# Three blocks on one core: modulation chunks redistributed around three passages from a norm to its transposes

## The chip, the cores and the metric

The kernel runs on one core of one Trainium2 chip. The metric is device time in microseconds (us) of one execution. Before the change it is 1364.03 us, the median of three runs (1363.72 to 1364.52).

## The reference

The input `x` is 256 tokens by 1024 columns, all in float32. A first block updates it by a mixer, a cross attention to 256 memory tokens and a SwiGLU feed-forward layer, each behind an RMS norm. A second block then runs twice, with its own weights for each of its two layers `l`: a mixer of four parts, and a mixture of 32 experts in groups. Cut to the part that matters here:

```python
mod = silu(c) @ w_ada[l] + b_ada[l]          # 1024 -> 6 x 1024
sh1, sc1, g1, sh2, sc2, g2 = split(mod, 6)
h = rms(x) * norm_mix_g[l] * (1 + sc1) + sh1
x = x + g1 * token_mixer(h, ...)
h = rms(x) * norm_ffn_g[l] * (1 + sc2) + sh2
x = x + g2 * hierarchical_moe(h, ...)
```

The modulation `mod` depends on `c` alone, not on `x`. So its product with `w_ada` (two layers of 1024 by 6144) can be computed at any time before its use.

## The kernel before, in words

**Stages.** In the order of the program: mixer 1, memory attention (`mem_attn`), feed-forward (`ffn`), then for l = 0 and l = 1 the mixer (`mixer2`) and the experts (`moe`), and a last norm. At the start of each stage a norm (`normed`, lines 355 to 364) turns `x` into scaled rows `xn`, half on DVE (line 363) and half on ACT (line 364). `to_T` (line 378) transposes them on TensorE in 16 pieces of 128x128, and ACT and DVE evacuate the pieces into `hT`, each as a high and a low part (lines 383 and 384 in `ffn`, lines 389 to 394 in the mixers). The passage from a norm to these transposes happens three times with work of the modulation nearby: n3 in `ffn`, and n4 in each of the two mixers.

**Products.** A float32 product is made of three matmuls of rounded parts (`mm3`, lines 277 to 279: high by high, high by low, low by high; called a triple below). The weights are split into the two parts on ACT (line 239, `whi`) and DVE (line 241, `wlo`). A product of 128 output rows over the 1024 rows of `hT` takes eight triples.

**Chunks.** `ada` (line 1032) computes the modulation as a generator: for each layer three groups `g`, and for each group eight chunks of `w_ada`, 128x2048 or 1 MB each, 48 in all. A chunk is a load on SP's queue (line 1053) and four matmuls (line 1055). When a group's eight are done, ACT copies its row (line 1060), TensorE makes four transposes (line 1067) and for g > 0 sixteen small matmuls (line 1078), and DVE adds biases (lines 1063, 1069 and 1081). This is called the mod row's work. `fill(n)` lets the generator go n steps at the place in the program where it is called, and `need(l, g)` runs it until a group is there. The table `FILL` (line 124) says how many steps are made where: 10 in `mem_attn` and one more behind it, 10 in `ffn` ahead of `to_T`, 12 in the first mixer ahead of `to_T`, none there in the second, and 7 and 8 within the main loops of the two mixers.

**Loads.** Loads of weights are issued by SP in the order of its queue, each into one of the 8 KB places (per partition) that `wtile` hands out in rotation. A load waits on SP until its place is free, and everything behind it on SP waits with it. In `moe` the places make a ring of slots of three (gate, up and down weights of an expert). `moe` ends with a branch (line 1864) to code for overflowing experts (`overflow`, line 1892 its loop), which has memory of its own.

**Order.** Each engine works its instructions in program order. The framework's scheduler may place a call's instructions ahead of those of an earlier call that wait for data; what results is seen in the order below.

Of the kernel before, what the change touches and what calls it, by code (L numbers as in the profile page):

```python
# [15 lines left out]
P = 128  # L16
S = 256
D = 1024
KT = 8
# [101 lines left out]

FILL = {"mem": 1, "ffn": 10, "mix0": 12, "mix": (7, 8)}

ORDER = (2, 0, 3, 1)

# [11 lines left out]
class Net:  # L139
# [280 lines left out]
    def build(self):  # L420
        ctx, tc, nc = self.ctx, self.tc, self.nc
        pool = lambda n, b, **k: ctx.enter_context(tc.tile_pool(name=n, bufs=b, **k))
        self.cst = pool("cst", 1)
        self.places = []
        self.ring, self.rest = [], []
        self.wctx = ctx.enter_context(ExitStack())
        self.kept = [self.more_places(self.wctx, "wst", 3), self.more_places(self.wctx, "wstb", 2)]
        self.per = pool("per", 1)
        self.junk = pool("junk", 1)
        self.psum = pool("psum", 8, space=bass.MemoryType.PSUM)  # L430
        x = self.per.tile([P, 2, D], F32, name="x")
        xs = self.A["x"][0].rearrange("(t p) d -> p t d", p=P)
        nc.sync.dma_start(x[:, 0], xs[:, 0])
        nc.scalar.dma_start(x[:, 1], xs[:, 1])
        self.x = x
        for tt in range(2):
            for h in range(2):
                self.x_done(tt, h)
        self.mhalf = self.cst.tile([P, 8], F32, name="mhalf")
        nc.gpsimd.memset(self.mhalf, -0.5)  # L440
        con = self.cst.tile([P, NCON1], F32, name="con")
        nc.scalar.dma_start(con, self.A["consts"][:, :NCON1])
        par = self.cst.tile([P, NPAR], F32, name="par")
        nc.scalar.dma_start(par, self.A["params"])
        self.C = {k: con[:, o:o + w] for k, (o, w) in CCOLS.items() if o < NCON1}
        self.V = {k: par[:, o:o + w] for k, (o, w) in PCOLS.items()}
        self.ident = self.C["ident"]
        o = CCOLS["upto"][0]
        self.upto_ones = con[:, o:o + 256]
        self.filler, self.ready = self.ada(), -1  # L450
        self.block1()
        if self.stop == "b1":
            return
        self.block2()
# [485 lines left out]
    def ffn(self):  # L940
        tc, nc, V, A = self.tc, self.nc, self.V, self.A
        v, act, te = nc.vector, nc.scalar, nc.tensor
        c, (self.whl, pf) = self.scope(("whl2", 4), ("pf", 1))
        with c:
            xn = self.normed(pf, "n3")
            self.fill(FILL["ffn"])
            hT = self.hpair(pf)
            win, wout = A["w_ffn_in"][0], A["w_ffn_out"][0]
            NJ = 11
            chunks = []  # L950
            for j in range(NJ + 1):
                if j < NJ:
                    chunks += [(win[:, j * 256:(j + 1) * 256], KT, 256, "n"),
                               (win[:, 2816 + j * 256:2816 + (j + 1) * 256], KT, 256, "n")]
                if j:
                    chunks += [(wout[(j - 1) * 256:j * 256, :], 2, D, "k")]
            hs = self.halves(chunks)
            self.to_T(xn, V["g_ffn_pre"], out=hT)
            ob = self.ob = [[self.bank("ob") for _ in range(2)] for _ in range(2)]

            def down(j, hid):
                for k in range(2):
                    W = next(hs)
                    for tt in range(2):
                        for half in range(2):
                            self.mm3(ob[tt][half], hid[:, k, tt * P:(tt + 1) * P], W[:, 0, half * 512:half * 512 + 512],
                                     j == 0 and k == 0, j == NJ - 1 and k == 1)

            pend = None
            for j in range(NJ + 1):  # L970
                if j < NJ:
                    bks = []
                    for _ in range(2):
                        bk = self.bank()
                        for f in range(2):
                            self.feat(bk[:, f * S:(f + 1) * S], next(hs), 0, P, hT)
                        bks.append(bk)
                if pend:
                    down(*pend)
                    pend = None  # L980
                if j < NJ:
                    bg, bu = bks
                    th = pf.tile([P, 512], F32, name="th", bufs=2)
                    act.activation(th, bg, AF.Tanh, scale=0.5)
                    v.scalar_tensor_tensor(th, th, 1.0, bg, op0=OP.add, op1=OP.mult)
                    v.scalar_tensor_tensor(th, th, 0.5, bu, op0=OP.mult, op1=OP.mult)
                    hid = Split(pf.tile([P, 2, S], F32R, name="hidh", bufs=2), pf.tile([P, 2, S], F32R, name="hidl", bufs=2))
                    t = th.rearrange("p (f t) -> p f t", f=2)
                    act.activation(hid.hi, t, AF.Copy)
                    v.tensor_tensor(hid.lo, t, hid.hi, op=OP.subtract)  # L990
                    pend = (j, hid)
            ss = self.sum_sq(pf, "o3")
            for h in range(2):
                ss.add(h, slice(h * 512, h * 512 + 512), [ob[0][h], ob[1][h]])
            self.post(pf, ss, "g_ffn_post")
        self.dump("x3", self.x)
# [35 lines left out]
    def ada(self):  # L1032
# [3 lines left out]
        nc = self.nc  # L1036
# [5 lines left out]
        for l in range(2):  # L1042
# [6 lines left out]
            for g in range(3):  # L1049
                bk = self.bank("ada")  # L1050
                for k in range(KT):
                    w = self.wtile()
                    nc.sync.dma_start(w, self.A["w_ada_2"][l][k * P:(k + 1) * P, g * 2048:(g + 1) * 2048])
                    for q in range(4):
                        te.matmul(bk[q * 32:(q + 1) * 32, :], cact[:, k:k + 1].to_broadcast([P, 32]),  # L1055
                                  w[:, q * 512:(q + 1) * 512], start=k == 0, stop=k == KT - 1)
                    if k < KT - 1:
                        yield
                row = self.per.tile([P, 512], F32, name="modrow")
                act.activation(row, bk, AF.Copy)  # L1060
                if g:
                    sl = slice(0, 64) if g == 1 else slice(64, 128)
                    v.tensor_tensor(grow[sl], grow[sl], bk[sl], op=OP.add)
                yield
                bk = self.bank()
                for c in range(4):
                    nc.tensor.transpose(bk[:, c * P:(c + 1) * P], row[:, c * P:(c + 1) * P], self.ident)
                cols = lambda t, o: t[:, o + g * 16:o + (g + 1) * 16].rearrange("p (q c) -> p c q", q=4)
                v.tensor_tensor(cols(self.mod[l], 0), bk.rearrange("p (c q r) -> p c q r", c=4, q=4)[:, :, :, 0],
                                cols(self.V["b_ada_2"], l * 48), op=OP.add)  # L1070
                if g:

                    bk = self.bank()
                    twin = row.rearrange("p (i k) -> p k i", k=8)
                    for k in range(8):
                        for h in range(2):
                            q = (2, 0)[g - 1] + h
                            te.matmul(bk[h * 64:h * 64 + 64, k:k + 1], twin[:, k], self.ident[:, q * 32:q * 32 + 1],
                                      start=True, stop=True)
                    o = (16, 40)[g - 1]  # L1080
                    v.tensor_tensor(self.mod[l][:, o:o + 8], bk[:, :8],
                                    self.V["b_ada_2"][:, l * 48 + o:l * 48 + o + 8], op=OP.add)
                self.ready = 3 * l + g

    def need(self, l, g):

# [15 lines left out]
    def mixer2(self, l):  # L1102
        tc, nc, V, C = self.tc, self.nc, self.V, self.C
# [4 lines left out]
        with c:  # L1108
# [8 lines left out]
            with tc.tile_pool(name="pxn2", bufs=1, reuse_waits="tile") as pxn:  # L1117
                xn = self.normed(pxn, "n4")
                with self.behind(2):
                    nc.gpsimd.dma_start(wdt, A["w_dt"][l])  # L1120
                    nc.gpsimd.dma_start(con2, self.A["consts"][:, NCON1:])
                    nc.gpsimd.dma_start(self.wr, A["w_router"][l])
                self.fill(FILL["mix0"] if l == 0 else 0)
                self.need(l, 0)
                self.retire(lambda p: p in self.kept)
                mod = self.mod[l]
# [5 lines left out]
                hs = self.halves([(win[:, c0:c0 + 256], KT, 256, "k" if c0 in (1800, 2824) else "n") for c0 in cols]  # L1132
                                 + [(wo[i], 2, D, "k" if n < 3 else "n") for n, i in enumerate(ORDER)])
                self.to_T(xn, ga, b=mod[:, 0:8], out=hT)
                self.free = 3
            self.top.close()

# [522 lines left out]
    def moe(self, l):  # L1660
# [209 lines left out]
        if l == 0:  # L1870
# [3 lines left out]
            a, b = self.places[4:], self.places[1:4]  # L1874
            self.places = (b + a if low else a + b) + self.places[:1]
            self.top = ExitStack()
        self.dump("x5_%d" % l, x)

    def overflow(self, l, pm, xn, ga, bb, comb, rank, sel):
# [84 lines left out]
```

## Time and profile before

| | |
|---|---|
| time, median of 3 runs | 1364.03 us (1363.72 to 1364.52) |
| the profiled execution's own time | 1362.82 us |
| its span, first to last instruction | 1360.9 us |
| mean granted TensorE clock | 0.957 of full |
| busy: TensorE / DVE / ACT / POOL | 92% / 52% / 41% / 6% |
| DMA moved | 375.93 MB, mean 276 GB/s |

The span leaves out what lies around the first and last instruction, here 1.9 us. A busy TensorE may run at its full clock or at half of it; the granted clock tells which. In the rows below a time is in us from the span's start, the brackets give the idle time of the engine ahead of a row and what ended it, and a count such as x40 counts the passes of the hardware, two for each float32 matmul.

### The profile page before, as it was taken

The numbers are of one execution on the slowest core, as the hardware profiler recorded it, in microseconds if no ns is written. First come the engines' busy times: TensorE is split into PE (matmuls) and PEld (weight loads), VectorE is DVE, ScalarE is ACT, GpSimd is POOL, SyncE is SP. The second block draws the span as 40 slices with busy tenths as digits, with TensorE's granted clock in tenths as the row PEclk, the third lists the DMA queues.
The fourth block names the chain that finished last, engine by engine and source line by source line (L and its number), as shares of the span: only waits on it lengthen the run. The fifth ranks groups of instructions, "written<-read, shape, count | busy, mean of one in ns | idle before, by whom it ended". The sixth has DMA issues, their size and how long they took to land. (4 is left out here: it accounts for less than half of the span.)

```text
span 1360.9 us, 26539 instructions
## 1 busy us (share of the span) xinstructions
PE 1246.7 (92%) x11058; PEld 999.5 (73%) x11058; DVE 702.4 (52%) x1414; ACT 552.3 (41%) x1022; POOL 76.8 (6%) x91
## 2 busy tenths in 40 slices
PE   6999999999999999999989977788999989978886
PEld 6988899866999995788876645465888877645553
DVE  5797756545555554686563322225685553332324
ACT  5578546544444443445532211114345532211212
POOL 2000000000000001122100000001122100000000
PEclk9998999999999998999989999888999989998988
DMA  9553448769955555864368999999563476999994
GB/s 313 166 180 96 167 159 275 303 269 379 365 201 188 186 186 180 296 228 152 142 278 364 418 418 419 418 420 336 175 229 139 171 279 281 418 418 418 418 418 181
DMA packets 131946, 375.93 MB, mean 276 GB/s; under 512 B 7056, under 2 KB 90128, under 8 KB 100848
## 3 DMA queue, kind: packets, MB, share of 16 engines
q1 hardware_dynamic: 130080, 367.84, 71.8%
q0 software_dynamic: 1312, 5.21, 1.0%
q8 instruction: 90, 1.47, 0.4%
q10 hardware_dynamic: 432, 1.14, 0.2%
q14 instruction: 32, 0.26, 0.1%
HBM read 373.12 MB, written 1.05 MB: 275 GB/s over the span
## 5 line engine op out<-in xcount | busy, mean ns | idle before, releaser
L241 DVE TENSOR_TENSOR wlo<-w,whi 128x1024 fp32r<-128x1024 f32 x214 | 263.0, 1231 | 190.0 <-ACT whi L239 189.7
L239 ACT ACTIVATE whi<-w 128x1024 fp32r<-128x1024 f32 x214 | 225.7, 1057 | 269.4 <-PE bk L278 181.2
L277 PE MATMUL bk<-hTh,whi 128*128 128x256 f32 (+1 forms) x1128 | 321.8, 287 | 2.7 <-ACT whi L239 2.5
L278 PE MATMUL bk<-hTl,whi 128*128 128x256 f32 (+1 forms) x1128 | 317.2, 282 | 0.9 <-DVE hTl L384 0.7
L279 PE MATMUL bk<-hTh,wlo 128*128 128x256 f32 (+1 forms) x1128 | 316.3, 281 | 0.3 <-DVE wlo L241 0.2
L277 PEld LDWEIGHTS bk<-hTh,whi 128*128 128x128 f32 (+1 forms) x1128 | 211.5, 188 | 21.4 <-issue 4.1
L1631 PE MATMUL bk<-w,XT 128*32 128x256 f32 (+1 forms) x2816 | 178.1, 410 | 44.9 <-DMA w<-in_w_up 41.0
L278 PEld LDWEIGHTS bk<-hTl,whi 128*128 128x128 f32 (+1 forms) x1128 | 210.9, 187 | 3.4 <-DVE hTl L384 1.2
L279 PEld LDWEIGHTS bk<-hTh,wlo 128*128 128x128 f32 (+1 forms) x1128 | 210.8, 187 | 2.0 <-DVE kk L1421 0.8
L1631 PEld LDWEIGHTS bk<-w,XT 128*32 128x32 f32 x2816 | 100.2, 118 | 121.6 <-issue 72.6
L1760 PE MATMUL bk<-Sg,xn 128*128 128x128 f32 x704 | 90.1, 285 | 4.3 <-DVE Sg L1740 4.3
L1760 PEld LDWEIGHTS bk<-Sg,xn 128*128 128x128 f32 x704 | 87.6, 201 | 6.8 <-issue 5.3
L1815 PE MATMUL bk<-w,hd 128*32 x704 | 79.8, 593 | 9.1 <-DMA w<-in_w_down 5.4
L1803 ACT ACTIVATE hd<-bk 128x256 f32<-128x256 f32 x22 | 8.4, 384 | 192.3 <-PE bk L1801 192.3
L1766 DVE TENSOR_SCALAR XT<-bk,gp,modcol 128x128 f32<-128x128 f32 x88 | 36.1, 410 | 87.3 <-PE bk L1760 79.0
L1822 ACT ACTIVATE oh<-od 128x512 fp32r<-128x512 f32 x44 | 27.7, 629 | 88.0 <-DVE od L1821 88.0
L1815 PEld LDWEIGHTS bk<-w,hd 128*32 128x32 f32 x704 | 23.4, 110 | 53.2 <-issue 49.6
L1793 DVE SCALAR_TENSOR_TENSOR mth<-mth,cslot,bk 128x256 f32<-128x256 f32 x22 | 10.6, 481 | 90.6 <-PE bk L1631 90.6
L1764 ACT ACTIVATE XT<-bk,modcol,gp 128x128 f32<-128x128 f32 x88 | 40.1, 456 | 37.0 <-DVE XT L1766 37.0
L1055 PE MATMUL ada<-w,cact 128*32 128x512 f32 x384 | 52.4, 654 | 1.0 <-DMA w<-in_w_ada 1.0
L1821 DVE TENSOR_TENSOR od<-bk,gb 128x512 f32<-128x512 f32 x44 | 30.2, 687 | 36.0 <-PE bk L1815 36.0
L1823 DVE TENSOR_TENSOR ol<-od,oh 128x512 fp32r<-128x512 f32 x44 | 30.4, 691 | 31.6 <-ACT oh L1822 31.5
(511 smaller groups left out, 1938.1 us busy)
## 6 DMA issues: line engine op xcount, KB each, us to landing
w<-in_w_gate SPq DMA_DIRECT2D x64, 1024.0 KB, 19.9
w<-in_w_up SPq DMA_DIRECT2D x64, 1024.0 KB, 19.9
w<-in_w_down SPq DMA_DIRECT2D x64, 1024.0 KB, 19.9
w<-in_w_in SPq DMA_DIRECT2D x48, 1024.0 KB, 6.6
w<-in_w_ada SPq DMA_DIRECT2D x48, 1024.0 KB, 5.0
w<-in_w_ffn_in SPq DMA_DIRECT2D x22, 1024.0 KB, 11.5
w<-in_w_out SPq DMA_DIRECT2D x12, 1024.0 KB, 5.3
w<-in_w_ffn_out SPq DMA_DIRECT2D x11, 1024.0 KB, 6.8
```

Source lines behind the costliest of these rows:

```text
L239: self.nc.scalar.activation(W.hi, v, AF.Copy)
L241: self.nc.vector.tensor_tensor(W.lo, v, W.hi, op=OP.subtract)
L277: mm(out, l.hi, r.hi, start=start, stop=False)
L278: mm(out, l.hi, r.lo, start=False, stop=False)
L279: mm(out, l.lo, r.hi, start=False, stop=stop)
L1055: te.matmul(bk[q * 32:(q + 1) * 32, :], cact[:, k:k + 1].to_broadcast([P, 32]), w[:, q * 512:(q + 1) * 512], start=k == 0, stop=k == KT - 1)
L1631: self.nc.tensor.matmul(out[ps, :S], XT[:, k, ps], w[i][:, k * S:(k + 1) * S], start=k == 0, stop=k == KT - 1)
L1760: te.matmul(o, xn[:, tt, d], Sg[:, tt], start=tt == 0, stop=tt == 1)
L1764: act.activation(XT[:, d], o, AF.Identity, scale=gp[:, d:d + 1], bias=bp[:, d:d + 1])
L1766: v.tensor_scalar(XT[:, d], o, gp[:, d:d + 1], bp[:, d:d + 1], op0=OP.mult, op1=OP.add)
L1815: te.matmul(bks[h][ps, :], hd[:, f, ps], wds[i][:, f * D + h * 512:f * D + h * 512 + 512], start=f == 0, stop=f == 1)
L1823: v.tensor_tensor(o.lo, t, o.hi, op=OP.subtract)
```

## The change

`FILL` gives two numbers for each passage: steps ahead of `to_T` and steps behind it. In `ffn` these are 4 and 6; in the mixer of layer 0 they are 3 and 5, in that of layer 1 they are 1 and 4; the main loops get 11 and 3 steps. A new `preload(n)` issues the loads of the next n chunks without their matmuls; the mixers call it for all chunks of the passage, after they have sorted the places so that those that outlive the passage come last. For layer 1 the end of `moe` adds five more places (`wst3`). No arithmetic changes: there are 48 chunks before and after.

```diff
-FILL = {"mem": 1, "ffn": 10, "mix0": 12, "mix": (7, 8)}
+FILL = {"mem": 1, "ffn": (4, 6), "mix0": ((3, 5), (1, 4)), "mix": (11, 3)}
...
+        self.todo, self.chunks = [(l, g, k) for l in range(2) for g in range(3) for k in range(KT)], []
...
             xn = self.normed(pf, "n3")
-            self.fill(FILL["ffn"])
+            self.fill(FILL["ffn"][0])
             hT = self.hpair(pf)
...
             self.to_T(xn, V["g_ffn_pre"], out=hT)
+            self.fill(FILL["ffn"][1])
...
                 for k in range(KT):
-                    w = self.wtile()
-                    nc.sync.dma_start(w, self.A["w_ada_2"][l][k * P:(k + 1) * P, g * 2048:(g + 1) * 2048])
+                    if not self.chunks:
+                        self.preload(1)
+                    w = self.chunks.pop(0)
...
+    def preload(self, n):
+
+        for _ in range(n):
+            l, g, k = self.todo.pop(0)
+            w = self.wtile()
+            self.nc.sync.dma_start(w, self.A["w_ada_2"][l][k * P:(k + 1) * P, g * 2048:(g + 1) * 2048])
+            self.chunks.append(w)
...
-                self.fill(FILL["mix0"] if l == 0 else 0)
+                few, more = FILL["mix0"][l]
+
+                self.places.sort(key=lambda p: p[0] in self.kept)
+                self.preload(few + more)
+                self.fill(few)
                 self.need(l, 0)
...
                 self.to_T(xn, ga, b=mod[:, 0:8], out=hT)
+                self.fill(more)
                 self.free = 3
...
             self.top = ExitStack()
+            self.more_places(self.top, "wst3", 5)
```

The changed file's lines lie 3 to 16 further down: the chunks' matmuls are line 1058 there (1055 before), their load line 1093 (1053), the mod row's work lines 1070 and 1081 (1067 and 1078), and the overflow branch line 1880 (1864).

First place, TensorE at n3 in `ffn`: `ada` is the accumulator of the chunks, `cact` the activated `c`, `modrow` the row of a finished group, `n3xn` the scaled rows; a chunk is four matmuls, so x20 is five chunks. Before:

```order
L1055 MATMUL ada<-w,cact 32x512 x20
L1067 MATMUL bk<-con,modrow 128x128 x4
L1078 MATMUL bk<-con,modrow 64x1 x16
L1055 MATMUL ada<-w,cact 32x512 x20
L378 MATMUL bk<-con,n3xn 128x128 x16
L277 MATMUL bk<-hTh,whi 128x256
```

And of the change:

```order
L1058 MATMUL ada<-w,cact 32x512 x20
L378 MATMUL bk<-con,n3xn 128x128 x16
L1070 MATMUL bk<-con,modrow 128x128 x4
L1081 MATMUL bk<-con,modrow 64x1 x16
L1058 MATMUL ada<-w,cact 32x512 x20
L277 MATMUL bk<-hTh,whi 128x256
```

The 16 transposes have moved ahead of the mod row's work and of five chunks; five chunks stay ahead of them. At n4 of layer 0 it is alike: three chunks, the transposes, the mod row's work, five chunks, where three chunks, the mod row's work, eight chunks, another mod row's transposes (line 1067), one chunk and the transposes stood. Four chunks and that line 1067 go on into the mixer's main loop. Between the transposes and the dt rows (line 1290) stand 32 triples, before and after.

Second place, TensorE behind the experts of layer 0, at n4 of layer 1. Before:

```order
L1864 UNCONDITIONAL_BRANCH x2
L378 MATMUL bk<-con,n4xn 128x128 x16
L277 MATMUL bk<-hTh,whi 128x256 x2
L278 MATMUL bk<-hTl,whi 128x256
L279 MATMUL bk<-hTh,wlo 128x256
```

And of the change:

```order
L1880 UNCONDITIONAL_BRANCH x2
L1070 MATMUL bk<-con,modrow 128x128 x4
L1081 MATMUL bk<-con,modrow 64x1 x16
L1058 MATMUL ada<-w,cact 32x512 x4
L378 MATMUL bk<-con,n4xn 128x128 x16
L1058 MATMUL ada<-w,cact 32x512 x4
L277 MATMUL bk<-hTh,whi 128x256
```

The mod row's work and one chunk now stand ahead of the transposes, a second chunk directly behind them, and three more among the triples ahead of the dt rows; before, all of this stood in the mixer's main loop.

Third place, SP's queue at the same norm, behind the same branch. Before:

```order
L1864 UNCONDITIONAL_BRANCH x2
L1053 DMA w<-in_w_ada 128x2048
L224 DMA w<-in_w_in 128x8x256
L1053 DMA w<-in_w_ada 128x2048
L224 DMA w<-in_w_in 128x8x256
```

And of the change:

```order
L1880 UNCONDITIONAL_BRANCH x2
L1093 DMA w<-in_w_ada 128x2048 x6
L224 DMA w<-in_w_in 128x8x256
L1093 DMA w<-in_w_ada 128x2048
L224 DMA w<-in_w_in 128x8x256
L1093 DMA w<-in_w_ada 128x2048
L224 DMA w<-in_w_in 128x8x256 x7
```

Six chunk loads stand ahead of the next load of the mixer's weights, where one did; four loads of these weights stand ahead of the branch in both. In the changed program the first of the six goes to memory that the overflow branch uses too, and waits for the events with which DVE and TensorE leave that branch; before, the first chunk load waited for a slot of the experts' ring alone.

## Rows read from the trace of the kernel before

**Rows 1.** The page, busy time, share of the span and instructions of each engine.
```profile
PE 1246.7 (92%) x11058; PEld 999.5 (73%) x11058; DVE 702.4 (52%) x1414; ACT 552.3 (41%) x1022; POOL 76.8 (6%) x91
```

**Rows 2.** Costliest groups: count, busy us, mean ns of one, idle us before them by releaser.
```profile
L1631 PE MATMUL bk<-w,XT 128*32 128x256 f32 (+1 forms) x2816 | 178.1, 410 | 44.9 <-DMA w<-in_w_up 41.0
```

**Rows 3.** Timeline at n3: start us, us, engine, line, operation, count, idle before.
```profile
316.30 4.50 PE L1055 MATMUL ada<-w,cact 128*32 128x512 f32 x40
...
322.29 0.66 PE L1067 MATMUL bk<-con,modrow 128*128 128x128 f32 x4 [1.49 <-ACT modrow L1060]
...
324.89 1.93 PE L1055 MATMUL ada<-w,cact 128*32 128x512 f32 x8
...
325.43 0.76 DVE L363 TENSOR_SCALAR n3xn<-x,n3y 128x1024 f32<-128x1024 f32 x1 [0.25 <-POOL n3y L356]
...
330.83 1.97 PE L378 MATMUL bk<-con,n3xn 128*128 128x128 f32 x16
...
332.56 0.36 PE L277 MATMUL bk<-hTh,whi 128*128 128x256 f32 x1
...
335.53 0.28 PE L277 MATMUL bk<-hTh,whi 128*128 128x256 f32 x1
...
337.99 0.28 PE L277 MATMUL bk<-hTh,whi 128*128 128x256 f32 x1
```

**Rows 4.** Timeline at n4 of layer 0, DVE and TensorE, up to line 1290.
```profile
519.50 2.78 PE L1055 MATMUL ada<-w,cact 128*32 128x512 f32 x24
...
530.11 0.75 DVE L363 TENSOR_SCALAR n4xn<-x,n4y 128x1024 f32<-128x1024 f32 x1 [0.88 <-POOL n4y L356]
...
537.77 0.66 PE L1067 MATMUL bk<-con,modrow 128*128 128x128 f32 x4 [0.79 <-ACT modrow L1060]
...
541.10 0.50 PE L277 MATMUL bk<-hTh,whi 128*128 128x256 f32 x2
...
556.46 0.28 PE L1290 MATMUL bk<-con,dtT 8*128 8x8 f32 x2
```

**Rows 5.** Timeline at n4 of layer 1, DVE and TensorE, up to line 1290.
```profile
937.19 0.63 PE L1831 MATMUL yb<-ol,ST 128*128 128x512 f32 x1
...
937.86 0.69 DVE L1861 TENSOR_TENSOR x<-x,yb 128x512 f32<-128x512 f32 x1 [0.16 <-PE yb L1831]
...
939.38 0.16 DVE L355 SCALAR_TENSOR_TENSOR n4y<-ssx 128x2 f32<-128x2 f32 x1 [0.83 <-ACTq L1864]
...
941.18 3.68 PE L378 MATMUL bk<-con,n4xn 128*128 128x128 f32 x16 [3.36 <-DVE n4xn L363]
...
944.50 0.78 PE L277 MATMUL bk<-hTh,whi 128*128 128x256 f32 x2
...
945.90 0.28 PE L278 MATMUL bk<-hTl,whi 128*128 128x256 f32 x1
...
959.40 0.29 PE L1290 MATMUL bk<-con,dtT 8*128 8x8 f32 x2
```

**Rows 6.** Stretches: length; busy PE, PEld, DVE, ACT, POOL; granted clock; DMA share; GB/s.
```profile
324.90:330.80 5.90, 5.90 (x42) 1.39 (x40) 3.29 (x4) 3.04 (x3) 0.50 (x1) 0.74 1.09 357
556.50:660.00 103.50, 102.42 (x892) 89.51 (x892) 73.09 (x126) 52.58 (x101) 18.59 (x17) 1.00 0.57 196
941.20:944.90 3.70, 3.70 (x18) 3.70 (x18) 1.93 (x5) 3.53 (x7) 1.11 (x3) 0.50 1.06 406
972.00:1070.00 98.00, 97.92 (x851) 83.42 (x849) 64.97 (x101) 47.82 (x93) 17.52 (x16) 0.98 0.56 196
```

**Rows 7.** Chunk loads of line 1053, all 48, from issue to landing.
```profile
DMA to landing us min/median/max: 4.7/5.0/15.5
```

**Rows 8.** DMA issues from 915 to 975 us: count, KB each, median us to landing.
```profile
w<-in_w_ada SPq DMA_DIRECT2D x4, 1024.0 KB, 7.9
```

**Rows 9.** Timeline of SP at the first experts, and of POOL ahead of n4.
```profile
717.48 1.28 SPq L1651 DMA_DIRECT2D w<-in_w_gate  x3
...
932.65 1.92 POOL L1431 MEMSET w<- 128x512 f32 x4 [236.35 <-PE bk L1815]
```

## The prediction

> **What bounds the kernel now.** I began with busy time by engine: TensorE works 1246.7 us of the 1360.9 us span, 92% [rows 1]. A change of order pays only where TensorE is idle, or runs at its lower clock. The chunks' matmuls are moved, not removed; what counts is what they cover.
>
> Next I read TensorE's timeline at the three norms. A warm matmul triple (lines 277 to 279) comes every 0.35 us: seven of them from 335.53 to 337.99. Five chunks on end take 4.50 us, 0.9 each [rows 3]. Ahead of the n3 transposes TensorE waits 1.49 us, then does the mod row's work (lines 1067 and 1078), five chunks and the transposes [rows 3]. At n4 of layer 0 it is the same with twelve chunks in all [rows 4]. At n4 of layer 1 no chunk is near: TensorE is idle for 3.36 us, and the 16 transposes take 3.32 us start to start, against 1.73 at n3 [rows 3, 5].
>
> The table of stretches tells why: granted clock 0.50 there, which is 1.2 GHz, and 0.74, half the time at that level, in the chunks behind the wait at n3 [rows 6]. In the mixers TensorE is idle for 1.08 and 0.08 us of some 100 [rows 6]: chunks put there cost their full time, and chunks taken out give it back.
>
> **Passage 1, n3.** No chunk is added or removed: five stand before the transposes as before, but the mod row's work and five chunks now stand behind them. The first five end at 320.80 as before. The scaled rows are ready when line 363 ends, 325.43 + 0.76 = 326.2 [rows 3], and TensorE is idle for 5.4 us until then. At half clock the transposes take 3.32 [rows 5], to 329.5. The mod row's work takes 322.29 to 324.89 = 2.60 [rows 3], to 332.1. Five chunks take 4.5 warm, or 324.89 to 330.83 = 5.94 as before [rows 3]: 336.6 or 338.0. They cover the evacuations (lines 383 and 384) and the weight splits, so dense triples follow at once. Before, triples ran dense from 335.53, with eight matmuls (0.9) done since 332.56 [rows 3]: the equal point is 334.6. So +2.0 to +3.4; I take the middle, **+2.7**, since the rows show clock lost behind such a wait, but no transposes ahead of such chunks. With transposes at full clock, 1.6 shorter (3.32 − 1.73), the low bound is +0.4.
>
> **Passage 2, n4 of layer 0.** Three chunks end at 519.50 + 2.78 = 522.3. The normalised rows are ready at 530.11 + 0.75 = 530.9 [rows 4]; so the transposes run to 534.2, the mod row's work to 536.8, five chunks to 541.3 or 542.7. Then 32 triples (11.2) lead to the dt rows of line 1290: 552.5 to 553.9, against 556.46 [rows 4], 4.0 to 2.6 earlier. That supposes that the five chunks cover all stalls behind the transposes: these were 556.46 − 541.10 − 11.2 − 0.2 (a quarter chunk) = 4.0; any part that stays is lost. But 12¼ chunks were done by line 1290, and now 8: 4¼ × 0.9 = 3.8 come later, and layer 1's line 1067 too, 0.66 [rows 4], in a mixer that has no room. Sum +0.5 to +1.9; middle **+1.2**. On SP's queue the first four w_in loads no longer stand behind twelve chunk loads; their splits run on ACT and DVE beside the wait, so I count nothing.
>
> **Passage 3, n4 of layer 1.** The mod row's work (2.60) starts when the MoE's last matmul ends, 937.19 + 0.63 = 937.8 [rows 5], and fits into the 3.36 us of idle time. One chunk then stands ahead of the transposes. Its load goes to memory that the overflow branch also uses, and the changed program holds it back until DVE and TensorE have left that branch. DVE's last add ends at 938.55, its next work starts at 939.38 [rows 5]: I put the issue at 939.0, between them. The median load lands after 5.0 us [rows 7], at 944.0; the chunk at half clock takes 1.8 (the one at 324.89 took 1.93 with its drain [rows 3]); the transposes run 945.8 to 949.1, where they ended at 944.50. Four chunks (3.6) and 32 triples (11.2) give 963.9. The stalls before were 959.40 − 944.50 − 11.2 = 3.7 [rows 5]; the chunks between the triples cover most, and I keep 1.0 of a possible 0 to 2. Line 1290 comes at 964.9, against 959.40: +5.5. In return five chunks (4.5) and the mod row's work (2.60) are gone from that mixer, 7.1. Sum **−1.6**, −2.6 to −0.6 by the stalls.
>
> The load's bounds: the shortest of all 48 took 4.7 (−0.3), the median in this stretch 7.9, where DMA is busy throughout (+2.9) [rows 7, 8]. Six chunk loads now stand ahead of the fifth w_in load, where one did; the first four w_in hold 64 triples, 22 us, which hide that one. POOL's memset of line 1431, 1.92 us [rows 9], moves behind its three DMA issues, which come earlier by nothing, since they wait for the norm; it costs nothing, as POOL idles for most of the mixer.
>
> **What reaches the end.** MoE is load-bound: TensorE waits 41.0 us for w_up [rows 2]. But its first five slots are filled ahead, and the next load starts at 717.48, when TensorE has let go of the first [rows 9]; a later mixer end shifts all of it, so I count 1:1.
>
> Sum: 2.7 + 1.2 − 1.6 = **+2.3 us** on the profiled execution's 1362.82, 1365.1. That execution lies 1.21 below the median of the runs, 1364.03; so the forecast is 1366.3. A measurement of this kernel tells 0.2%, 2.7 us, from no change: the forecast lies just within.
>
> **Rivals.** *Faster: the waits cost less.* The transposes and the chunks behind them keep full clock in the first two passages: +0.4 and 0.5 − 1.6 = −1.1. In passage 3 the chunk's data is there in time, the chunk runs in the idle time, and the transposes end 4.6 earlier: −1.6 − 4.6 = −6.2. Together −6.9: 1357.1; with passage 3 alone, 1366.3 − 4.6 = 1361.7. For it: the stalls behind the transposes (4.0 and 3.7) are real, and chunks now stand in them. Against: idle time grows from 1.49 to 5.4 us at n3, the clock had fallen after less [rows 3, 6], and the queue ties the load to the branch's end. Chance 0.27.
>
> *Slower: the late chunk load.* TensorE runs in order, so transposes, evacuations and all of the mixer stand behind the chunk. If it lands after 7.9 us instead of 5.0, passage 3 turns from −1.6 to +1.3 and the sum is +5.2: 1369.2. It decides from 0.4 us on, at a landing of 5.4. For it: DMA is full in this stretch [rows 6], six loads are issued at once, and the constants' 1 MB come in beside them. Against: the four w_in loads should have landed by then. Chance 0.17.
>
> *Slower: the clock stays down behind the transposes.* After the cold transposes the matmuls come slowly from 944.50 on, 1.4 us long, and are warm at 945.90 [rows 5]; so the transposes seem to have counted. The Trainium skill, "TensorE: Matmul & The Clock Gate", Part 4 (PE-mode transpose), says the reverse: transposes don't count as busy in the way matmuls do. By it the chunks behind them would start cold; the row speaks against most of that rule. As a mechanism here: the upper ends in passages 1 and 2 (+3.4, +1.9), and in passage 3 two of the four chunks 0.7 longer each (−0.2): +5.1, 1369.1. For it: the transposes are followed by the mod row's small matmuls, behind which the chunks were cold before too [rows 3]. Chance 0.12.
>
> *No effect.* MoE's load bound, or stalls elsewhere, take up what the mixers gain or lose: 1364.0. Against it is the slot release [rows 9]. Chance 0.07.
>
> **The numbers.** My forecast has 0.37, somewhat over half of it within 0.2%, the rest slower, since +2.3 stands near the edge and its terms spread from −0.1 (lower ends) to +4.7. With the rivals: faster 0.25 (nearly all of the first), same 0.37 (a part of the forecast, all of no effect, the mild forms of each rival), slower 0.38. The range reaches to 1358.5 and 1370.5, nearly to the first rival's full price below and past both slower rivals above. The likeliest case's own range is 1363.9 to 1368.7.
>
> **What would show it.** Right: TensorE idle for some 5.4 and 8.6 us ahead of the n3 and n4 transposes, these at clock 0.50, no stall behind; in passage 3 a wait of some 3.5 us for a chunk's load, transposes ending near 949; the mixer of layer 0 some 4 us longer, that of layer 1 some 7 shorter. Wrong: full clock in the transposes, or layer 1's chunk inside the idle time (faster); its load at 8 us or more, or cold triples behind the chunks (slower).

## The result: 0.7% slower

The change takes 1373.33 us, the median of five runs (1370.94 to 1375.47), against 1363.72 of the five runs of before beside them. The ratio is 1.0072, with an interval of 1.0061 to 1.0083: 9.6 us slower, where +2.3 was forecast and the range ended at 1370.5. A repeat gave 1374.04 against 1362.88 (ratio 1.0086, 1.0069 to 1.0104). The profiled execution took 1374.75 us, its span 1372.9.

I cut the span at five marks which both traces have, and took the stage lengths between them. The feed-forward stage runs from the last product of the memory attention to its own last one, mixer 0 from there to the experts' first gather, the experts to their last matmul, and mixer 1 from there to the next gather:

| stretch, us | before | after | difference | forecast |
|---|---|---|---|---|
| up to the first mark | 316.4 | 317.5 | +1.2 | 0 |
| feed-forward, with n3 | 203.2 | 208.9 | +5.7 | +2.7 |
| mixer 0, with n4 of layer 0 | 187.5 | 188.9 | +1.4 | +1.2 |
| experts 0 | 230.7 | 230.3 | −0.4 | 0 |
| mixer 1, with n4 of layer 1 | 182.9 | 186.6 | +3.7 | −1.6 |
| experts 1 | 229.8 | 230.6 | +0.8 | 0 |

The first line is the same program in both; over all the kernels below it lay between 315.3 and 317.9. Mixer 0, where its program is that of before, took 187.4 to 188.7 us in eight profiles and 190.7 in a ninth. So a difference of a single profile under some 3 us is not read as the change's. The feed-forward stage and mixer 1 carry the loss, and each missed its forecast.

**At n3**, TensorE's timeline of the change answers to [rows 3] (columns as there; lines 1058, 1070 and 1081 are 1055, 1067 and 1078 of before):

```profile
317.46 4.50 PE L1058 MATMUL ada<-w,cact 128*32 128x512 f32 x40
327.40 3.85 PE L378 MATMUL bk<-con,n3xn 128*128 128x128 f32 x16 [5.45 <-DVE n3xn L363]
331.05 1.06 PE L1070 MATMUL bk<-con,modrow 128*128 128x128 f32 x4
332.04 2.09 PE L1081 MATMUL bk<-con,modrow 128*64 128x1 f32 x32
334.06 7.39 PE L1058 MATMUL ada<-w,cact 128*32 128x512 f32 x40
341.38 0.39 PE L277 MATMUL bk<-hTh,whi 128*128 128x256 f32 x1
```

The idle time ahead of the transposes is 5.45 us, as forecast. But the transposes, the mod row's work and most of the five chunks run slowly: the chunks take 7.39 us instead of 4.50. From the end of the first five, 317.46 + 4.50, to the dense triples it is 19.4 us; before it was 13.8 to the equal point. The stretches say why, and show n4 of layer 0 beside it (columns as in [rows 6]):

```profile
327.40:331.00 3.60, 3.60 (x16) 3.39 (x17) 1.36 (x3) 2.23 (x5) 0.00 (x0) 0.50 1.10 351
331.00:334.00 3.00, 3.00 (x38) 2.67 (x36) 2.60 (x6) 3.00 (x6) 0.00 (x0) 0.50 1.03 395
334.00:341.40 7.40, 7.40 (x44) 1.69 (x43) 4.16 (x6) 2.04 (x4) 0.00 (x0) 0.60 1.08 363
537.80:541.40 3.60, 3.60 (x17) 3.39 (x18) 2.27 (x4) 3.41 (x6) 3.04 (x7) 0.51 0.68 217
541.40:550.00 8.60, 8.60 (x91) 5.18 (x90) 6.21 (x20) 5.00 (x11) 0.00 (x0) 1.00 0.78 260
```

The clock stood at 0.50 through transposes and mod row's work, and 0.60 as the mean over the chunks says that it rose only in their last fifth. In n4 of layer 0 it was back ahead of the chunks, which take 4.50 ([rows 4] answer to this; line 1306 is 1290 of before):

```profile
526.37 2.78 PE L1058 MATMUL ada<-w,cact 128*32 128x512 f32 x24
537.80 3.75 PE L378 MATMUL bk<-con,n4xn 128*128 128x128 f32 x16 [8.64 <-DVE n4xn L363]
541.38 0.60 PE L1070 MATMUL bk<-con,modrow 128*128 128x128 f32 x4
...
543.93 4.50 PE L1058 MATMUL ada<-w,cact 128*32 128x512 f32 x40
...
559.88 0.28 PE L1306 MATMUL bk<-con,dtT 8*128 8x8 f32 x2
```

There the transposes end the wait of 8.64 us at half clock, 537.80 to 541.38, and no stall follows: from the stage's start to the dt rows it is 33.4 us, against 36.9 before.

**At n4 of layer 1**, SP (its row first) and TensorE answer to [rows 5]:

```profile
947.07 3.27 SPq L1093 DMA_DIRECT2D w<-in_w_ada  x6
...
945.07 0.63 PE L1847 MATMUL yb<-ol,ST 128*128 128x512 f32 x1
947.03 1.11 PE L1070 MATMUL bk<-con,modrow 128*128 128x128 f32 x4 [1.33 <-DVEq L1880]
948.07 2.09 PE L1081 MATMUL bk<-con,modrow 128*64 128x1 f32 x32
951.90 1.94 PE L1058 MATMUL ada<-w,cact 128*32 128x512 f32 x8 [1.74 <-DMA w<-in_w_ada]
953.76 3.68 PE L378 MATMUL bk<-con,n4xn 128*128 128x128 f32 x16
957.37 1.22 PE L1058 MATMUL ada<-w,cact 128*32 128x512 f32 x8
...
961.16 1.06 PE L1058 MATMUL ada<-w,cact 128*32 128x512 f32 x8 [1.66 <-DMA w<-in_w_ada]
...
975.35 0.29 PE L1306 MATMUL bk<-con,dtT 8*128 8x8 f32 x2
```

The first chunk's load is issued at 947.07 and its matmuls start at 951.90. The transposes start 8.1 us behind the experts' last matmul (945.07 + 0.63), 3.4 before; and 961.16 shows a second wait of 1.66 us, for the third chunk's load. The dt rows come 29.7 us behind the experts, 21.6 before: +8.1. The main loop then gives back 4.4 of it (161.3 to 156.9), where I had counted 7.1. Its waits, in the view of who waited for whom, between line 1306 and the experts:

```profile
PE bk L1320 <- DVE la L1318: 2.3, 1, 2.3
PE bk L1479 <- DVE w L1471: 1.2, 1, 1.2
```

Before, line 1304 (1320 of the change) waited 1.0, and line 1463 (1479) is not in this view:

```profile
PE bk L1304 <- DVE la L1302: 1.0, 1, 1.0
```

### The profile page after: what moved, and what is told of

It is laid out like the page before. It is cut to its first block, busy times and chain, and to the rows that moved or that the text cites. A ratio compares the mean times of both kernels' runs of the same rounds, so it can differ in the third digit from the quotient of the medians.

```text
span 1372.9 us, 26537 instructions
## 1 busy us (share of the span) xinstructions
PE 1245.4 (91%) x11058; PEld 998.1 (73%) x11058; DVE 705.5 (51%) x1414; ACT 552.9 (40%) x1022; POOL 79.2 (6%) x91
```

## The experiments

Theory A: what counts is idle time, half clock and late loads at the passages; chunks are moved but not for free, since they also covered something where they stood. Theory B: layer 1's late load is all of it. Theories C and D are named where they are tried. Where the code below is the change's, a condition `if more:` also skips the sorting and the early issue where no step stands behind the transposes.

**One passage alone, three kernels.** The table `FILL` sets the others as before; the third has the five places, the first two don't.

```diff
-FILL = {"mem": 1, "ffn": (4, 6), "mix0": ((3, 5), (1, 4)), "mix": (11, 3)}
+FILL = {"mem": 1, "ffn": (4, 6), "mix0": ((12, 0), (0, 0)), "mix": (7, 8)}
...
+FILL = {"mem": 1, "ffn": (10, 0), "mix0": ((3, 5), (0, 0)), "mix": (11, 8)}
...
+FILL = {"mem": 1, "ffn": (10, 0), "mix0": ((12, 0), (1, 4)), "mix": (7, 3)}
```

> The change at n3 alone (4 steps ahead of the transposes, 6 behind), all else as before. Theory A (the passages themselves cost what the two traces show): transposes, mod row's work and most of the five chunks at granted clock 0.50, dense triples 5.6 us later, time +3 to +6 us. Theory B (only the load of layer 1's chunk matters; what n3 loses is made up in the feed-forward layer): within 1 us of before.

> The change at n4 of layer 0 alone (3 and 5 steps, 11 in its main loop, so that layer 1 is as before). Theory A: the dt rows come some 3.4 us earlier, the mixer's main loop takes it back with 4 chunks and one line 1067 (4.4 to 4.8), time +0.5 to +2 us. Theory B: within 1 us of before. A third reading, that the clock is luck of the moment behind each wait, gives up to +4 where the clock stays at half behind these transposes too.

> The change at n4 of layer 1 alone (1 and 4 steps, 3 in its main loop, five more places). Theory A: the transposes end some 8 us later than before, the dt rows 8 us, the main loop gives back some 4, time +3 to +5 us. Theory B: all of the 9.6 us. My forecast of record: -1.6 us.

Measured, against 1363.18 us of before: n3 alone 1367.84 (ratio 1.0022, 1.0007 to 1.0036), n4 of layer 0 alone 1365.71 (1.0014, 1.0004 to 1.0024), n4 of layer 1 alone 1366.08 (1.0009, 0.9999 to 1.0018). The medians lie 4.7, 2.5 and 2.9 us up, 10.1 together; by the ratios it is 3.0, 1.9 and 1.2, 6.1 together, of the change's 9.8 or, in the repeat, 11.7. No single part carries the whole, so theory B falls. That the parts add up to it is not shown: the two sums differ by 4 us, and layer 1's ratio is not clear of no change; by it, theory A's +3 to +5 there is missed, and so is my record's −1.6. In the traces the stage of each got longer: feed-forward +4.1, mixer 0 +3.4, mixer 1 +5.4 (+3.8 in a second profile). Of mixer 0's extra 2 us against the change's +1.4, 1.5 come from its main loop (157.0 against 155.5 us) and 0.5 from the passage (34.0 against 33.4), where the mod row's transposes ran at half clock too; the mended kernel below has that main loop as well.

**Both sides.** Another split, to see whether the idea pays at other numbers:

```diff
+FILL = {"mem": 1, "ffn": (7, 3), "mix0": ((8, 4), (0, 0)), "mix": (7, 8)}
```

> Another split: n3 with 7 steps ahead and 3 behind, n4 of layer 0 with 8 and 4, layer 1 as before, no chunk moved to another stage. Theory A (what counts is idle time and clock at the passages; work ahead keeps TensorE busy until the rows are ready, a few chunks behind cover the evacuations): -2 to -5 us against before. Theory C (any gap ahead of the transposes costs the clock, whatever stands behind): 0 to +3 us.

Measured: 1366.09 us (1.0015, 1.0004 to 1.0027); theory A's gain did not come. The time lies in theory C's range, but not for its reason: the transposes kept full clock at both norms, 1.97 us for the 16. At n3 the stage became 2.2 us shorter (201.0), at n4 of layer 0 it became 4.1 longer. The timeline of TensorE and ACT there shows a wait that I had not thought of:

```profile
529.72 1.97 PE L378 MATMUL bk<-con,n4xn 128*128 128x128 f32 x16
531.61 2.78 PE L1058 MATMUL ada<-w,cact 128*32 128x512 f32 x24
539.04 1.11 PE L1070 MATMUL bk<-con,modrow 128*128 128x128 f32 x4 [4.64 <-ACT modrow L1063]
...
536.83 1.06 ACT L239 ACTIVATE whi<-w 128x1024 fp32r<-128x1024 f32 x1 [3.40 <-DMA w<-in_w_in]
...
538.41 0.58 ACT L1063 ACTIVATE modrow<-ada 128x512 f32<-128x512 f32 x1
```

The three chunks behind the transposes end a group. The mod row's transposes behind them need ACT's copy (line 1063); on ACT that stands behind a weight split (line 239) which waits 3.40 us for a w_in load. TensorE waits 4.64 us for the copy. The n3 split alone was tried further on.

**Kept busy at n3.** The change at n3 alone, with idle work in TensorE's wait:

```diff
             self.fill(FILL["ffn"][0])
+            hold = self.bank("hold")
+            for _ in range(HOLD):
+                nc.tensor.matmul(hold[:, :P], self.ident, self.ident, start=True, stop=True)
...
+HOLD = 24
```

> The change at n3 alone, with 24 matmuls of 128x128 whose result nothing reads put into TensorE's idle time ahead of the transposes (about 5.2 us of work at full clock in a wait of 5.5). Theory A (the clock is what n3 loses): transposes and chunks behind them at full clock, 1.8 and 4.5 us; from the end of the first five chunks to dense triples some 4 us less than with the change at n3 alone; time 0 to +1 us against before. Theory D (the order itself costs, by the evacuations or the mod row's work): the same +3 to +5 us as the change at n3 alone.

Measured: 1364.04 us against 1363.30 (1.0003, 0.9994 to 1.0013). The loss at n3 is gone. The timeline, with `hold` as the idle work (line numbers one to four further down than the change's):

```profile
321.83 5.62 PE L951 MATMUL hold<-con 128*128 128x128 f32 x48
327.44 2.16 PE L379 MATMUL bk<-con,n3xn 128*128 128x128 f32 x16
329.43 0.60 PE L1074 MATMUL bk<-con,modrow 128*128 128x128 f32 x4
...
331.98 4.50 PE L1062 MATMUL ada<-w,cact 128*32 128x512 f32 x40
336.41 0.38 PE L278 MATMUL bk<-hTh,whi 128*128 128x256 f32 x1
```

And the stretches:

```profile
322.00:327.40 5.40, 5.40 (x48) 5.26 (x48) 4.21 (x8) 3.54 (x10) 0.71 (x1) 1.00 1.09 365
327.40:332.00 4.60, 4.60 (x56) 4.22 (x56) 3.33 (x5) 4.60 (x9) 0.00 (x0) 1.00 1.08 359
332.00:337.00 5.00, 5.00 (x47) 1.77 (x46) 4.60 (x10) 2.38 (x5) 0.00 (x0) 1.00 1.06 366
```

But for the idle work, the order is that of n3 alone; the transposes and the five chunks now run at full clock, 2.16 and 4.50 us, and the stage is 204.0 us instead of 207.3. Theory A holds at n3, theory D falls.

**The first load early.** The change at n4 of layer 1 alone, with the first chunk's place taken from the experts' ring:

```diff
                     self.places.sort(key=lambda p: p[0] in self.kept)
+                    if l:
+                        self.places.insert(0, self.places.pop())
+                        self.places.append(self.places.pop(5))
```

> The change at n4 of layer 1 alone, but the first chunk's place is one of the experts' ring, so that its load stands ahead of the overflow branch on SP's queue. Theory A (late load, cold clock and uncovered waits together): TensorE doesn't wait for a chunk's load ahead of the transposes, which start some 6 us after the experts' last matmul instead of 8; time 2 us less than with the change there alone, still 0 to +2 us against before. Theory B (the late load is all of it): transposes some 4.6 us earlier, time -2 to 0 us against before.

Measured: 1363.27 us against 1363.30, but the ratio of 1.0015 has an interval of 1.0000 to 1.0029: seven of the twelve runs lay at 1361.8 to 1363.7 and five at 1367.4 to 1368.2. The time does not show the 2 us that were expected: by the ratio this kernel is no faster than with the late load (1.0009). In the trace the transposes start 6.3 us behind the experts instead of 8.1, and the stage is 183.2 us, +0.3 against before.

**Chunks left out.** The kernel before without five of layer 1's chunks; this leaves out part of the modulation of that layer.

```diff
-                for k in range(KT):
+                for k in range(5 * (l * g == 2), KT):
...
+FILL = {"mem": 1, "ffn": (10, 0), "mix0": ((12, 0), (0, 0)), "mix": (7, 3)}
```

> The kernel before with the first five chunks of layer 1's last group left out, loads and matmuls, and nothing put in their place; the last three stand at the first three places of layer 1's main loop. My record: a chunk is worth 0.9 us in the mixer, the main loop gets 4.5 us shorter. Theory A: the chunks covered waits there, so the main loop gets only 1.5 to 3 us shorter, with new waits of TensorE for DVE.

Measured: 1358.60 us against 1363.30 (0.9967, 0.9956 to 0.9978), 4.5 us by the ratio. So a chunk is worth its 0.9 us there within the interval of 3.0 to 6.0, and theory A's 1.5 to 3 asks too little. In the profile the main loop is 6.2 us shorter. Its waits in that main loop, which answer to those of the change above:

```profile
PE bk L1480 <- DVE w L1472: 1.2, 1, 1.2
PE bk L1321 <- DVE la L1319: 1.0, 1, 1.0
```

Line 1480 has its new 1.2 us with the chunks gone; line 1321 keeps its 1.0 where the mod row's work still stands in this loop. In the change that work is gone too, and this wait is 2.3. The two waits grew by 2.5 us together, close to the 2.7 that the main loop did not give back. But they do not settle the sum: the change with n3 kept busy, further on, has the same order and the same two waits in this loop and gave back 8.1 us, and the mended kernel, again with both waits, 2.1.

**n3 with 7 and 3 steps alone.**

> At n3 alone 7 steps ahead of the transposes and 3 behind. Theory A: TensorE idles for little ahead of the transposes, these keep their clock, three chunks cover the evacuations: -1 to -3 us. Theory C (any chunk behind the transposes costs): 0 to +2 us.

Measured: 1363.26 us against 1363.30 (0.9999, 0.9988 to 1.0010). Neither theory's gain nor loss is shown; the interval, −1.6 to +1.4 us, reaches into both ranges. The stage is 0.4 us shorter here and was 2.2 shorter with the same order in the profile above: there the two chunks ahead of the transposes took 1.92 us, here 3.24 at a mean clock of 0.57. It was the version nearest to a gain, and is none.

**The change again, mended, and before kept busy.** Three kernels side by side: the change once more; the change with idle work at n3 (24 matmuls) and at n4 of layer 0 (39), and the first load early; and before with 7 idle matmuls in each of its three waits.

```diff
             self.fill(FILL["ffn"][0])
+            self.hold(24)
...
+                if l:
+                    self.places.insert(0, self.places.pop())
+                    self.places.append(self.places.pop(5))
                 self.preload(few + more)
                 self.fill(few)
+                if l == 0:
+                    self.hold(39)
```

> The change itself once more, on the chip of the two runs beside it. Theory A: +8 to +10 us; the low stretch of the clock at n3 is there again, though its length may differ (it was 13.7 us in the first profile, 10.2 with the change at n3 alone). If the low stretch were chance alone, it would be missing, with some 5 us less.

> The change with three causes taken out: 24 idle matmuls in the wait at n3, 39 in the wait at n4 of layer 0, and layer 1's first chunk load ahead of the overflow branch. Theory A (clock at n3 4, late load 2 to 5, clock at n4 of layer 0 some 2): 7 to 10 us less than the change, so -1 to +2 us against before. Theory D (the moved chunks themselves cost): at least +4 us stay.

> The kernel before with 7 idle matmuls in each of its three waits (ahead of the mod row's work at n3 and at n4 of layer 0, ahead of the transposes at n4 of layer 1). Theory A (half clock behind these waits costs, and a busy TensorE keeps it): the chunks behind the first two waits take 4.5 instead of 5.9 and 7.2 instead of 9.9 us, transposes of layer 1 up to 1.7 us less: -3 to -6 us. Rival (the clock falls by what follows, the mod row's small matmuls, or is low already from the experts' end): -1 to +1 us.

Against 1362.88 us of before: the change 1374.04 (1.0086), mended 1366.17 (1.0022, 1.0013 to 1.0032), before kept busy 1364.52 (1.0011, 1.0000 to 1.0022). The repeat shows the slow stretch at n3 again, with chunks of 5.78 us instead of 7.39. Mending takes 7.9 of the 11.2 us away, as theory A said; 3.3 stay, more than its +2. At n4 of layer 0 the idle work brought little: it lasted beyond the wait, so the transposes start 13.0 us into the stage instead of 11.4, at full clock, and the dt rows come 0.2 us earlier than in the change's first profile. The last kernel missed, with +1.5 by the ratio against −3 to −6 of theory A and −1 to +1 of its rival: its timeline (line 1058 the chunks, 1102 the idle work) shows the gain that was expected at n3, and none at n4 of layer 1:

```profile
321.04 1.83 PE L1102 MATMUL hold<-con 128*128 128x128 f32 x14
...
325.25 4.50 PE L1058 MATMUL ada<-w,cact 128*32 128x512 f32 x40
329.68 1.97 PE L378 MATMUL bk<-con,n3xn 128*128 128x128 f32 x16
...
939.49 3.35 PE L1102 MATMUL hold<-con 128*128 128x128 f32 x14 [1.33 <-DVEq L1891]
942.63 2.01 PE L378 MATMUL bk<-con,n4xn 128*128 128x128 f32 x16
```

The chunks behind the first wait take 4.43 us start to start (325.25 to 329.68) instead of 5.94 [rows 3]. At n4 of layer 1 the idle work runs at half clock itself and pushes the transposes to 942.63, 4.5 us behind the experts instead of 3.4; what these win by their clock is spent. At n4 of layer 0 the chunks took 8.77 us, not 7.2, and the stage got 2.1 us longer, which is within what one profile tells. So idle work mends a loss that the change had made at n3, and no gain over before is shown.

**One cause out of the whole change.** The change with the idle work at n3 alone, and the change with the first load early alone, each by its edit above. What was open then: how much of layer 1's loss is the load, since the two profiles of that passage came from different groups of runs. So that passage, with the load late and early, was profiled once more.

> The whole change with the 24 idle matmuls at n3 alone. Theory A: the clock at n3 is worth 4 to 5 us, so +5 to +7 us against before are left. If the clock lost at n3 is only lost later instead, +9 or more stay.

> The whole change with layer 1's first chunk load ahead of the overflow branch, nothing else. Theory A by the two profiles of that passage: 3 to 5 us less than the change, +6 to +8 us left. By the timed runs of that passage alone (1366.1 and 1363.3 us, in two groups each): 0 to 3 us less.

> The change at n4 of layer 1 alone, another profile. Its runs lay in two groups, near 1363.4 and near 1366.5 us; the first profile was of the upper. Theory A: a profile of the lower group shows the passage as before (first chunk near 6 us behind the experts' end, transposes near 8) and fewer us at half clock behind them; if the late load makes the groups, it shows an earlier load.

> The same passage with its first load early, another profile. Its runs lay near 1362.5 and near 1367.8 us; the first profile was of the lower group. Theory A: a profile of the upper group shows the transposes at the same 6.3 us behind the experts' end, and the 5 us as half clock or as waits behind them.

Against 1362.78 us: 1367.59 with n3 kept busy (1.0036, 1.0021 to 1.0052) and 1371.23 with the early load (1.0061, 1.0037 to 1.0084). Beside the change's 1.0086 these are some 7 and some 3 us less; beside its 1.0072 some 5 and 1.5. So with n3 kept busy 4.9 us are left by the ratio (2.9 to 7.1), where theory A had +5 to +7. With the early load 8.3 are left (5.0 to 11.4); this interval overlaps the change's, so in time the load's part is not clear of noise. SP and TensorE of the kernel with the early load:

```profile
941.34 0.34 SPq L1093 DMA_DIRECT2D w<-in_w_ada  x1
...
945.29 0.63 PE L1850 MATMUL yb<-ol,ST 128*128 128x512 f32 x1
947.24 1.12 PE L1070 MATMUL bk<-con,modrow 128*128 128x128 f32 x4 [1.32 <-DVEq L1883]
...
950.31 1.94 PE L1058 MATMUL ada<-w,cact 128*32 128x512 f32 x8
952.18 3.15 PE L378 MATMUL bk<-con,n4xn 128*128 128x128 f32 x16
...
961.09 1.07 PE L1058 MATMUL ada<-w,cact 128*32 128x512 f32 x8
```

The load is issued at 941.34, ahead of the experts' end; the chunk follows the mod row's work without a wait, and the transposes start 6.3 us behind the experts. The wait for the third chunk's load (961.09) is gone as well. In each of the five profiles with the late load these two waits make 3.3 to 4.9 us together; in the four with the early one no chunk of this passage waits for its load.

Mixer 1 as a stage was 186.6, 186.6 and 186.7 us in three profiles with the late load (the change twice, the passage alone again), and 183.3, 183.2 and 183.2 in three with the early one: 3.4 us. Three further profiles lie apart: with the late load the passage alone at first with 188.3 and the change with n3 kept busy with 183.0, and with the early one the mended kernel with 184.8. The first took 23.2 us from the transposes to the dt rows (21.5 in its second profile), the others 153.3 and 159.2 us in the main loop (156.9 to 157.1 in the rest). For the 153.3 the trace shows the clock: the first 20 us behind the dt rows, in the change and in the change with n3 kept busy (columns as in [rows 6]), and the two waits of the latter's main loop:

```profile
975.40:995.40 20.00, 17.75 (x121) 15.63 (x121) 11.67 (x29) 6.39 (x10) 4.71 (x4) 0.83 0.61 203
971.60:991.60 20.00, 17.69 (x153) 16.32 (x152) 14.19 (x33) 8.54 (x14) 4.71 (x4) 1.00 0.64 212
PE bk L1323 <- DVE la L1321: 2.3, 1, 2.3
PE bk L1482 <- DVE w L1474: 1.2, 1, 1.2
```

At 0.83 instead of 1.00, 3.4 us of full-clock work are lost in 20 us, nearly all of the 3.7 between 156.9 and 153.3; before had 0.91 there. Why the clock fell in the one and not in the other, behind the same order, stays open. So does what makes the two groups of runs of a kernel: neither of the two profiles taken for it was of the group it was meant for (1366.31 and 1359.45 us).

## Why the prediction was wrong

**Passage 1 failed by its clock.** I took the middle between warm and partly cold chunks, +2.7, with +3.4 as the upper end: "the rows show clock lost behind such a wait, but no transposes ahead of such chunks". It measured +5.7 in the first profile and in that of the change with the early load, and +4.1 in two more (n3 alone, and the repeat); with TensorE kept busy +0.8. In the two of +4.1 the chunks were near what my upper end had (5.71 us start to start against 5.94), and 0.7 came on top: transposes of 3.64 us where I took 3.32, and mod row's work of 3.02 where I took 2.60. That price is from a stretch at a mean clock of 0.94 behind a wait of 1.49 us, and the work now stood behind one of 5.45. In the first profile the chunks took 7.32, slower than I had allowed for. So the mechanism of the term was right and its size half to two thirds of what came; that it is the clock is shown by the idle work, in the passage alone and in the whole change. Not all that the idle work won at n3 reached the end: mixer 0 was 3.4 to 3.5 longer than before in that profile and in the repeat, and 1.4 in the two where n3 had lost 5.7. Over both stages it won 2.9 to 3.4 us.

**Passage 2 held in the first profile, and not in most others.** +1.2 was forecast, +1.4 measured there. The dt rows came 3.5 us earlier as a part of the stage (4.0 to 2.6 forecast), and the main loop paid 4.9 (4.5 forecast). Of the four other profiles with this passage one has +1.4 too; the repeat has +3.5 and two more +3.4, with nearly the same passage (33.9 us in the repeat) and 157.0 to 157.1 of main loop, where the clock fell once more. My sum had no term for that. Since the unchanged mixer 0 took 190.7 us once, the change's share in it is open.

**Passage 3 failed behind the transposes, not ahead of them.** The wait for the load was forecast to 0.1 us: transposes 8.0 us behind the experts, 8.1 measured. That was luck in part: I let the mod row's work start at the experts' end, and it started 1.33 us later, behind the branch; the late chunk hid it. Wrong were two steps behind the transposes. "Four chunks (3.6) and 32 triples (11.2)" with 1.0 us of stalls make 15.8 us; from 957.37 to 975.35 it took 18.0. Of these 2.2 us, 1.66 are the third chunk's load, which I had left out, as I priced only the first. And "five chunks (4.5) and the mod row's work (2.60) are gone from that mixer, 7.1": 4.4 came back. Two waits of TensorE for DVE grew there by 2.5 us, and the first 20 us of the loop ran at 0.83 of full clock instead of 0.91. Of the nine profiles with this order in the main loop, all with both waits, seven gave back 4.2 to 4.4, one 2.1 and one 8.1. The last kept its clock, so the waits alone are not the cause; what share each has is open. I had read 0.08 us of idle time in that mixer [rows 6] as a sign that nothing is covered there. But the stretch read begins at 972.00, behind the wait of line 1304 at 967.7. And where TensorE never waits, some of what it does may be the cover.

**The rivals.** The late chunk load did not come true as I had put it: the first chunk's matmuls start 4.8 us behind the issue (947.07 to 951.90), where that rival wanted a landing past 5.4. The load held TensorE up as the forecast had it, and a second time at the third chunk. With both waits gone mixer 1 is 0.3 to 0.4 us longer than before in three profiles, and 1.9 in the mended kernel's. *Faster* had a price out of reach in passage 3: with the early load the transposes still start 6.3 us behind the experts, not 3.4. The clock that stays down came true at n3 and not at n4 of layer 0. The rule of the Trainium skill that stood behind it ("TensorE: Matmul & The Clock Gate", Part 4: PE-mode transpose, transposes don't count as busy in the same way) agrees with n3, where the clock rose only among the chunks, and not with n4 of layer 0 in the first profile, where it was full at 541.40, with the 16 transposes alone behind the wait. I ended the range just past either slower rival's price; what came was more than either had at n3, with the two terms of passage 3 on top. *No effect* is out: in the change the experts' lengths are those of before within 0.8 us (experts 0 up to 1.9 shorter in other profiles), so they pass on most of what the mixers gain or lose, as I had read from the slot release.

**What is left.** With the three causes mended, 3.3 us remain: mixer 0 is 2.7 longer than before, mixer 1 1.9 and the feed-forward stage 0.8, and experts 0 1.9 shorter. In mixer 0 the main loop is 157.0 us against 150.6. The chunks and the line moved there are worth 4.5 by the forecast's prices; for the rest, the first stretch of that loop shows a slow clock:

```profile
555.00:575.00 20.00, 18.88 (x150) 16.63 (x151) 12.27 (x31) 8.14 (x13) 2.23 (x3) 0.91 0.56 179
```

A mean of 0.91 over 20 us, where before and the change's first profile had 1.00, is some 3.6 us at half clock, or 1.8 us lost. The same stretch of the repeat had 0.91 as well. Why it fell there in some profiles and not in others was not tried, so the 3.3 us are explained in part only.

## What to carry to other kernels

Work that fills the wait ahead of a step can do two things: it uses the time, and it can keep TensorE's clock, as the idle work did at n3. Moving it behind the step can give up both, so price the slow clock over everything up to where it rises again, not over the step alone. And when loads are queued ahead into new memory, look at who owned that memory last: the first load may wait for the end of an engine's branch, and an in-order TensorE stands still behind it.

## What the runs showed that I had not expected

- The same order gave different clocks. After a wait of 5.45 us at n3, transposes and mod row's work ran at half clock and so did the first of the chunks, which took 5.78 or 7.39 us for five; after one of 8.64 us at n4 of layer 0 the clock was full again once the transposes were done in two profiles, and in three more only among the mod row's small matmuls. The order of before had both too: behind a wait of 1.5 us at n3 its five chunks took 5.9 to 6.2 us in six profiles and 4.50 in a seventh, without idle work.
- Idle matmuls of 128x128 without any use held the clock through the whole wait at n3 (1.00 in all of it), and behind 7 of them ahead of the mod row's work in the kernel before the chunks at n3 ran at full clock, those at n4 of layer 0 not. They did not pay in time there.
- Before the first moved instruction, the same program differed by up to 2.6 us between profiles (315.3 to 317.9 us), and a mixer 0 that no edit had touched by up to 3.3; so one profile of each kernel does not decide about 0.2%.
